# Four Strassen pairs for one merge gate, and a row moved between two stages

## The chip, the cores and the metric

The kernel runs on one core of a Trainium2 chip. The metric is the time of one execution on the device in microseconds (us), taken as the median of several runs. A core has five engines that run side by side and wait for each other through semaphores: TensorE (PE, the matmuls; its weight loads are listed as PEld), VectorE (DVE), ScalarE (ACT), GpSimd (POOL) and SyncE (SP), which here only issues transfers between HBM and the on-chip memory. PSUM, the memory that the matmuls write, has 8 banks of 128 x 512 fp32. The profile is of one execution on the chip, and gives each instruction's start and duration.

## The reference

One decoder layer, 1024 tokens of 1024 channels, all in fp32:

```
h = RMSNorm(x)
s5_x | s5_gate | lru_x | lru_gate | gate_s | gate_l = h @ W_in     (512, 512, 1280, 1280, 1024, 1024 columns)
y_s = S5(s5_x); y_s = GLU(GELU(y_s) @ W_glu) * silu(s5_gate);      z_s = y_s @ W_bs
y_l = RGLRU(conv4(lru_x)) * silu(lru_gate);                        z_l = y_l @ W_bl
x = x + RMSNorm((sigmoid(gate_s) * z_s + sigmoid(gate_l) * z_l) @ W_out)
x = x + (p @ W_ple) * sigmoid(x @ W_ple_gate)
```

S5 is a diagonal complex state space model; RGLRU is a gated recurrence in ten heads of 128 channels, whose gates are r and i, with a = exp(c r), a multiplier sqrt(1 - a^2), and a scan over the tokens.

## The kernel before

**Matmuls.** Channels lie on the 128 partitions, tokens along the rows, in two halves of 512. A weight block is 128 x 128. Every operand is split into a high part (a rounded copy, made by ScalarE) and a low part (the rest, made by VectorE as a subtraction), and one block product is three matmuls of 128 x 512 (`three`, lines 327 to 331): high x high, high weight x low data, low weight x high data. A *row* (`rows`) is one block of 128 output columns over all 8 blocks of 1024 input channels and both halves of the tokens: 48 matmuls. W_in has 44 such columns: 0 to 3 s5_x, 4 to 7 s5_gate, 8 to 17 lru_x, 18 to 27 lru_gate, 28 to 35 gate_s, 36 to 43 gate_l.

**Strassen pairs.** Two columns m and m+1 together with two halves of the inputs and two of the tokens are a 2 x 2 block product, which `lprod` and what follows do in seven products of 12 matmuls instead of eight. The first product (B11) and the second (B21) accumulate in one bank X; then come T2, T1, T3, B22 and T4 into banks Z and W. T1 to T4 are sums of quarters of h, each built once for all pairs by `t_early` and `t_build` (VectorE subtracts, ScalarE makes the high part, VectorE the low part). Before the change gate_s has three pairs, at columns 30, 32 and 34, and plain rows for 28 and 29. The products with W_bl further on have the same shape (`bprod`, banks bX, bZ, bW, bV), where W_bl's channels 8 and 9 (of ten) are not in the 2 x 2 scheme and are added as *tails* (`btail`).

**Weights.** `weight_plan` writes out the order of all weight blocks; SP loads chunks of eight in that order. A chunk is used as two *quads* of four blocks. `W.ahead()` makes quads some places ahead of the one in use, in a ring of six: high part by ScalarE (L232), low part by VectorE (L245), or, for the quads in `LIGHT`, by a second ScalarE copy (L236) and an adding transfer that GpSimd issues (L237). A row uses two quads, a Strassen product one.

**Order.** There is no planner. Each engine takes its instructions in the order in which the program writes them. Side work is written as generators in a list `bg`; `tick()` advances each of them by one step, four times in a row and once after a product, and `drain()` runs them to the end.

**The stages around the change.** Behind the norm come the rows for S5's input (u), then twelve plain rows (4, 5, 36 to 43, 28, 29), beside which the S5 model runs as side work (`s5_all`: eight blocks, each with a few small matmuls and a Gelu at its end, `py` and `ysb`). Then the three pairs. Then ten LRU heads: for each the row lru_x (conv), the row lru_gate (silu), and two gate products per half of the tokens, which `between` calls inside the next row. What follows a head's gates is its `late`: Tanh, Exp, Square, Sqrt on ScalarE, two products, the scan and the product with silu on VectorE, giving yr0 to yr9. Behind the heads come the s5_gate rows 6 and 7 (`light` with silu), which have head 9's gates inside and its `late` beside them; then yl8 and yl9 are split, and the W_bl products begin: four B11 products, the tails, four B21 products, then the GLU (`ps_eb`, `ps_ea`, whose input `geo` is split from S5's outcome), and the rest of the W_bl products. The B21 operand is the split of four of the yr rows (`bB`).

Of the kernel before, what the change touches and what calls it, by code (L numbers as in the profile page):

```python
# [34 lines left out]
PAIRS = (30, 32, 34)  # L35


def weight_plan():
# [46 lines left out]
    gated(6, NL - 1)  # L85
    plain(col("w_in", 7, range(ND)))
    hi2 = range(8, NL)
    for ks in (lo, hi2, hi):
# [175 lines left out]
def tile_hybrid_trunk(  # L264
# [81 lines left out]
    def drain():  # L346
        while bg:
            tick()
# [769 lines left out]
    for m in range(2):  # L1118
        light(4 + m, sil_d[m], True, ev_tile)
    for m in range(ND):  # L1120
        light(36 + m, sgl_d[m], False, ev_tile)
    for m in range(PAIRS[0] - 28):
        light(28 + m, sgs_d[m], False, ev_tile)
# [24 lines left out]
    def lprod(ps, op, start):  # L1148
        W.ahead()
        for k, wb in enumerate(W.next()):  # L1150
            three(ps, wb, (op[0][:, k, :], op[1][:, k, :]), start and k == 0, k == 3, not start)

# [3 lines left out]

    wide_ctx.close()
    gps = gctx.enter_context(tc.tile_pool(name="gps", bufs=1, space=PSUM))

    def gbank(i, name):  # L1160
        return gps.tile([P, HT], F32, tag=f"gb{i}", name=name)

    bg.append(t_build())
    lu = quarter(page(9, "lu", F32))
    xs = [px.tile([P, HT], F32, tag="px", name=f"lX{p_}") if p_ < 2 else gbank(0, "lX2") for p_ in range(3)]
    for p_ in range(3):
        if p_ == 0:
            tick()
        lprod(xs[p_], hq["B11"], True)
        S.activation(lu[:, p_], xs[p_], AF.Copy)  # L1170
        tick()
    for p_, m in enumerate(PAIRS):
        o = gp.tile([P, NT], F32, tag="c", name=f"lo{p_}", bufs=2)[:, HALF[0]]
        lprod(xs[p_], hq["B21"], False)
        gate_out(m, 0, o, xs[p_])
        tick()
    for p_, m in enumerate(PAIRS):
        z = gbank(1 + p_, f"lZ{p_}") if p_ < 2 else px.tile([P, HT], F32, tag="px", name="lZ2")
        w_ = gbank(3 + p_, f"lW{p_}")
# [47 lines left out]
    def lru_head(m):  # L1227
# [22 lines left out]
        def gates(h):  # L1250
            if h == 0:
                held.extend(W.next())
            for t, b, bias in ((r, held[0], b_a), (i, held[1], b_x)):
                ps = px.tile([P, HT], F32, tag="px", name=f"pg{m}{h}")
# [66 lines left out]
    def gel_build():  # L1321
        for _ in range(3):
            yield
# [22 lines left out]
    def b21_ops():  # L1346
        bop("B21", 0, 1)
        for k in range(4):
            bsplit("B21", k, bq(21, k))
            if k % 2:  # L1350
                yield
# [505 lines left out]
```

## Time and profile before

| | |
|---|---|
| median of three runs | 920.82 us (920.50 to 920.89) |
| the profiled execution, and its span | 920.58 us, 918.8 us |
| TensorE, matmuls | 911.0 us busy, 99%, 4192 records |
| VectorE, ScalarE, GpSimd | 71%, 54%, 13% busy |
| rows beside S5 | about 69 to 235 us |
| the three pairs | 235 to 293 us |
| LRU heads and rows 6 and 7 | 293 to 559.8 us |
| first W_bl products (B11, tails, B21) | 559.8 to 587.0 us |

A row of the timeline gives start, duration (both us), engine, line of the program, operation, the tile written and the tiles read, the shape, and how many instructions the row joins; in square brackets stands how long the engine was idle before, and what ended that. A row of the waits gives the engine and its instruction, what it waited for, us in total, times, and the longest. Buffer numbers are left out of the names in the profile: `wq` is every quad of weights in the ring, `wraw` every loaded chunk, `lX` and `bX` are the banks of the first two products, `sg` the outcome of a Sigmoid row, `bB` a split operand of a W_bl product. Line numbers in the profile are those of the kernel before.

### The profile page before, as it was taken

Reading aid. Unit: us, or ns where it says so; the run is one execution under the profiler, and the core shown is the slowest. Engines: PE = TensorE matmul, PEld = TensorE weight load, DVE = VectorE, ACT = ScalarE, POOL = GpSimd, SP = SyncE. Lnnn points to the kernel's source line nnn. Section 1 sums busy time; section 2 is a strip of 40 time slices with the busy share of each in tenths; the row PEclk is TensorE's granted clock in tenths of the full one; section 3 lists DMA queues with packets and bytes.
Section 4 is the critical chain, followed back from the end, with each engine's and each line's share of the span. In section 5 each row is a group of like instructions: output and inputs, shape, how many; then the busy total and the mean of one; then the engine's idle time right before and its main releaser. Section 6 shows DMA issues by size and latency. Waiting matters only on the chain.

```text
span 918.8 us, 11750 instructions
## 1 busy us (share of the span) xinstructions
PE 911.0 (99%) x4192; PEld 754.0 (82%) x4192; DVE 656.6 (71%) x1068; ACT 494.6 (54%) x764; POOL 116.8 (13%) x129
## 2 busy tenths in 40 slices
PE   9999999999999999999999999999999999999998
PEld 7888888888788888888888888888888887887887
DVE  6978978796762356667666668687762798886863
ACT  6644255456754257776666668445433345558531
POOL 1211000011100000000000000021322126422100
PEclk9999999999999999999999999999999999999999
DMA  9785777668455101111111117811579965499961
GB/s 357 296 269 154 220 239 198 187 180 244 127 172 172 52 29 34 47 51 52 51 48 52 51 46 232 284 35 57 164 265 230 274 156 206 126 249 235 275 206 57
DMA packets 76298, 146.53 MB, mean 159 GB/s; under 512 B 18896, under 2 KB 33360, under 8 KB 76240
## 3 DMA queue, kind: packets, MB, share of 16 engines
q1 hardware_dynamic: 53216, 110.39, 36.0%
q10 hardware_dynamic: 16256, 22.55, 8.3%
q0 software_dynamic: 6768, 12.85, 7.8%
q8 instruction: 33, 0.54, 0.2%
q14 instruction: 25, 0.20, 0.1%
HBM read 101.06 MB, written 31.72 MB: 145 GB/s over the span
## 4 chain that ended last, share of the span: by engine, by line
PE 84%; issue 9%; DVE 2%; DMA 2%; POOL 2%; ACT 1%; POOLq 0%; ACTq 0%; DVEq 0%
PE ps_L L331 10%; PE ps_rg L331 8%; PE ps_rx L331 8%; PE ps_L L329 5%; PE ps_rx L329 4%; PE ps_rg L329 4%; PE ps_pg L331 3%; PE ps_u L331 3%; PE bZ L331 3%; PE ps_F L331 3%; PE bW L331 2%; PE bX L331 2%; PE pg L331 2%; PE lZ L331 2%; PE ps_ple L331 2%
## 5 line engine op out<-in xcount | busy, mean ns | idle before, releaser
L331 PE MATMUL ps_L<-hB,wq 128*128 128x512 f32 x448 | 138.1, 389 | 0.0
L232 ACT ACTIVATE wq<-wraw 128x512 fp32r<-128x512 f32 (+1 forms) x191 | 114.8, 614 | 42.4 <-DMA wraw<-w_blocks 15.3
L245 DVE TENSOR_TENSOR wq<-wraw,wq 128x512 fp32r<-128x512 f32 (+1 forms) x146 | 100.6, 704 | 15.0 <-ACT wq L232 14.9
L331 PE MATMUL ps_rg<-hB,wq 128*128 128x512 f32 x320 | 98.6, 389 | 0.0
L331 PE MATMUL ps_rx<-hB,wq 128*128 128x512 f32 x320 | 98.5, 389 | 0.0
L331 PEld LDWEIGHTS ps_L<-hB,wq 128*128 128x128 f32 x448 | 84.1, 188 | 17.4
L329 PE MATMUL ps_L<-hB,wq 128*128 128x512 f32 x224 | 88.1, 393 | 0.0
L331 PE MATMUL ps_pg<-x1hl,wq 128*128 128x512 f32 x240 | 74.6, 391 | 0.7 <-DVE x1hl L1533 0.5
L1237 DVE SCALAR_TENSOR_TENSOR c<-ps_rx,cp_t,c 128x1023 f32<-128x1023 f32 (+2 forms) x30 | 38.4, 1282 | 49.2 <-ACT c L1235 48.5
L331 PEld LDWEIGHTS ps_rx<-hB,wq 128*128 128x128 f32 x320 | 60.1, 188 | 12.6
L331 PEld LDWEIGHTS ps_rg<-hB,wq 128*128 128x128 f32 x320 | 60.1, 188 | 12.6
L329 PE MATMUL ps_rx<-hB,wq 128*128 128x512 f32 x160 | 62.2, 389 | 0.0
L329 PE MATMUL ps_rg<-hB,wq 128*128 128x512 f32 x160 | 62.2, 389 | 0.0
L237 POOL DMA_DIRECT2D wq<-wraw x45 | 39.6, 880 | 163.5 <-ACT wq L236 118.0
L204 POOL TENSOR_TENSOR wS<-wraw 128x512 f32<-128x512 f32 x8 | 12.4, 1547 | 333.5 <-DMA wraw<-w_blocks 326.1
L331 PEld LDWEIGHTS ps_pg<-x1hl,wq 128*128 128x128 f32 x240 | 44.8, 188 | 11.3 <-DVE x1hl L1533 1.4
L329 PEld LDWEIGHTS ps_L<-hB,wq 128*128 128x128 f32 x224 | 42.1, 188 | 8.5
L329 PE MATMUL ps_pg<-x1hl,wq 128*128 128x512 f32 x120 | 46.9, 391 | 0.0
L331 PE MATMUL ps_u<-hB,wq 128*128 128x512 f32 x128 | 39.8, 392 | 0.4 <-DVE hB L771 0.4
L331 PE MATMUL ps_F<-ys,wq 128*128 128x512 f32 x128 | 39.4, 389 | 0.0
L1245 ACT ACT_TABLE_LOAD x9 | 11.5, 1283 | 51.2 <-DVE yr L1274 51.2
L329 PEld LDWEIGHTS ps_rg<-hB,wq 128*128 128x128 f32 x160 | 30.0, 188 | 6.2
(394 smaller groups left out, 2071.3 us busy)
## 6 DMA issues: line engine op xcount, KB each, us to landing
wraw<-w_blocks SPq DMA_DIRECT2D x98, 512.0 KB
wq<-wraw POOLq DMA_DIRECT2D x45, 256.0 KB, 4.8
xt<-x_t SPq DMA_DIRECT2D x8, 512.0 KB
ple_d<-ple_sb SPq DMA_DIRECT2D x8, 512.0 KB
h_d<-xt SPq DMA_DIRECT2D x8, 512.0 KB
wn<-sbt ACTq DMA_DIRECT2D x8, 512.0 KB
wn<-pt_d ACTq DMA_DIRECT2D x16, 256.0 KB
fT<-h_d ACTq DMA_DIRECT2D x4, 1024.0 KB
```

The costliest lines, as they stand in the source:

```text
L204: (self.nc.vector if light else G).tensor_tensor(s[name], s[a], s[b], op)
L232: nc.scalar.activation(hi, src, AF.Copy)
L237: nc.gpsimd.dma_start(lo.bitcast(F32), src, accum_op=ALU.add)
L245: self.nc.vector.tensor_tensor(lo, src, hi.bitcast(F32), ALU.subtract)
L329: T.matmul(ps, wh, xh, start=start, stop=False, skip_group_check=more)
L331: T.matmul(ps, a, b, start=False, stop=stop and a is (wh if xl_last else wl), skip_group_check=more)
L1237: V.scalar_tensor_tensor(c[:, d:], ps[:, :NT - d], w_[3 - d], c[:, d:], ALU.mult, ALU.add)
L1245: S.activation(sq, ps, AF.Sigmoid)
```

## The change

Columns 28 and 29 become a fourth pair. The first products (B11) of all four pairs are written before the `drain()` that ends the S5 side work, in the order of `PORDER` (columns 32, 34, 28, 30), with the banks of two pairs in one wide tile; the second products follow, with `t_build` beside them. The s5_gate row 6 moves from behind the LRU heads to the rows beside S5, so that eleven rows and four first products stand there where twelve rows stood. Behind the heads only row 7 is left. Both halves of head 9's gates now stand in the middle of that row, and the first W_bl products are reordered: B11, then B21, then the tails; the B21 operand and yl8, yl9 are split beside the B11 products, and S5's outcome beside the B21 products.

```
-PAIRS = (30, 32, 34)
+BESIDE = (4, 5, *range(36, 39), 6, *range(39, 44))
+PORDER = (2, 3, 0, 1)
+PAIRS = (28, 30, 32, 34)
...
-    for m in (4, 5, *range(36, 44), *range(28, PAIRS[0])):
+    for m in BESIDE:
         plain(col("w_in", m, range(ND)))
-    first = [b for ks in (lo, hi) for m in PAIRS for b in col("w_in", m, ks)]
+    first = [b for ks in (lo, hi) for i in PORDER for b in col("w_in", PAIRS[i], ks)]
...
-    gated(6, NL - 1)
-    plain(col("w_in", 7, range(ND)))
+    gated(7, NL - 1)
     hi2 = range(8, NL)
-    for ks in (lo, hi2, hi):
+    for ks in (lo, hi, hi2):
...
+    for p_ in PORDER:
+        if p_ < 2:
+            xs[p_] = px.tile([P, HT], F32, tag="px", name=f"lX{p_}")
+        lprod(xs[p_], hq["B11"], True)
+        for i in ((), (2, 3), (0,), (1,))[PORDER.index(p_)]:
+            S.activation(lu[:, i], xs[i], AF.Copy)
+        tick()
     drain()
     s5x.close()
...
+    bg.append(t_build())
+    for n, p_ in enumerate(PORDER):
+        lprod(xs[p_], hq["B21"], False)
+        for i in ((), (2, 3), (0,), (1,))[n]:
+            o = gp.tile([P, NT], F32, tag="c", name=f"lo{i}", bufs=2)[:, HALF[0]]
+            gate_out(PAIRS[i], 0, o, xs[i])
+        tick()
     wide_ctx.close()
...
+    def between(q):
+        if q == 0:
+            last(0)
+            last(1)
+
+    light(7, sil_d[3], True, lambda name: l1.tile([P, NT], F32, tag="c", name=name, bufs=2), between=between)
     gel_load()
...
+    def tail_ops():
+        tail_split(8)
+        yield
+        bop("B21", 0, 1)
+        for k in range(4):
+            bsplit("B21", k, bq(21, k))
+            if k == 1:
+                yield
+        while 9 not in yl_raw:
+            yield
+        tail_split(9)
+
+    bg.append(tail_ops())
+    bu = quarter(page(19, "bu", F32))
+    x01 = wide("bX01")
+    xs = [x01[:, HALF[p]] if p < 2 else px.tile([P, HT], F32, tag="px", name=f"bX{p}") for p in range(4)]
+    for p_ in range(4):
+        bprod(xs[p_], "B11", True)
+        for i in ((), (0, 1), (2,), (3,))[p_]:
+            S.activation(bu[:, i, :], xs[i], AF.Copy)
+        tick()
+    drain()
...
     for p_ in range(4):
-        bprod(xs[p_], "B11", True)
-        S.activation(bu[:, p_, :], xs[p_], AF.Copy)
+        bprod(xs[p_], "B21", False)
         tick()
...
             btail(xs[2 * q + i], wb[2 * i:2 * i + 2], 0, False)
-        tick()
-    for p_ in range(4):
-        bprod(xs[p_], "B21", False)
-        brow(2 * p_, 0, gts[p_ // 2][:, HALF[p_ % 2]], xs[p_])
+        for p_ in (2 * q, 2 * q + 1):
+            brow(2 * p_, 0, gts[p_ // 2][:, HALF[p_ % 2]], xs[p_])
         tick()
```

How the instructions move is shown at three places. The lists give the program's order on one engine, without times; a number behind a name counts the buffer, and line numbers are somewhat higher in the changed kernel (L232 is L233 there).

ScalarE at the end of S5, before the change. `ysb7` is S5's last Gelu, `sg_29` the Sigmoid of the last plain row, `wq` quads of weights (a light one in two copies), `lu` the copies of the first products:

```order
L1016 ACT_TABLE_LOAD
L1016 ACTIVATE ysb7_2289<-py7_2290 128x512
L1020 DMA y_d_84<-ysb7_2289 8x16x128 x4
L1065 ACT_TABLE_LOAD
L1065 ACTIVATE sg_29_2304<-ps_L29_2209 128x1024
L1069 DMA sgs_d_80<-sg_29_2304 128x1024
L232 ACTIVATE wq40_2325<-wraw22_1946 128x512
L236 ACTIVATE wq40_2325<-wraw22_1946 128x512
L1170 ACTIVATE lu_2317<-lX0_2318 128x512
L232 ACTIVATE wq41_2346<-wraw22_1946 128x512
```

And now:

```order
L1138 ACTIVATE lu_2212<-lX23_2213 128x512 x2
L1095 ACTIVATE lT20_2261<-fT2_2054 128x512 x4
L233 ACTIVATE wq40_2267<-wraw22_1949 128x512
L237 ACTIVATE wq40_2267<-wraw22_1949 128x512
L1138 ACTIVATE lu_2212<-lX0_2266 128x512
L233 ACTIVATE wq41_2290<-wraw22_1949 128x512
L237 ACTIVATE wq41_2290<-wraw22_1949 128x512
L1138 ACTIVATE lu_2212<-lX1_2289 128x512
L1017 ACT_TABLE_LOAD
L1017 ACTIVATE ysb7_2315<-py7_2316 128x512
L1021 DMA y_d_84<-ysb7_2315 8x16x128 x4
L233 ACTIVATE wq42_2336<-wS2_42_2300 128x512
```

The light quads and the copies of the first products now stand ahead of S5's last Gelu.

ScalarE at head 9's gates, before. `r9` and `i9` are the Sigmoids of the two gates (`pg90` the first half of the tokens, `pg91` the second), `sq9` the Sigmoid of the lru_gate row, `ta9` the Tanh that begins `late`:

```order
L1245 ACTIVATE sq9_4257<-ps_rg9_4341 128x1024
L232 ACTIVATE wq110_4418<-wraw60_4182 128x512
L1256 ACTIVATE r9_4254<-pg90_4445,cp_t_97 128x512
L1256 ACTIVATE i9_4255<-pg90_4450,cp_t_97 128x512
L232 ACTIVATE wq111_4455<-wraw61_4221 128x512
L1256 ACTIVATE r9_4254<-pg91_4484,cp_t_97 128x512
L1256 ACTIVATE i9_4255<-pg91_4489,cp_t_97 128x512
L1065 ACTIVATE sg_6_4494<-ps_L6_4417 128x1024
L232 ACTIVATE wq112_4499<-wraw61_4221 128x512
L232 ACTIVATE wq113_4501<-wraw62_4301 128x512
L1262 ACTIVATE ta9_4256<-r9_4254,sp8_98 128x1024
```

And now:

```order
L1249 ACTIVATE sq9_4336<-ps_rg9_4420 128x1024
L233 ACTIVATE wq115_4497<-wraw62_4261 128x512
L1263 ACTIVATE r9_4333<-pg90_4524,cp_t_97 128x512
L1263 ACTIVATE i9_4334<-pg90_4525,cp_t_97 128x512
L1263 ACTIVATE r9_4333<-pg91_4534,cp_t_97 128x512
L1263 ACTIVATE i9_4334<-pg91_4534,cp_t_97 128x512
L233 ACTIVATE wq116_4543<-wraw63_4300 128x512
L233 ACTIVATE wq117_4545<-wraw63_4300 128x512
L1269 ACTIVATE ta9_4335<-r9_4333,sp8_98 128x1024
```

The four gate Sigmoids follow one another, and row 6's Sigmoid is gone from here.

VectorE from there to the W_bl products, before. `i9` by `ta9`, the scan into `sq9`, and `yr9` are the end of head 9; `sg_7` is row 7's silu, `yl8` and `yl9` the tails' operands, `bB211` the low part of the B21 operand; wq111 to wq114 are the four B11 weights, wq117 is B21's first:

```order
L1267 SCALAR_TENSOR_TENSOR ta9_4256<-sq9_4257,ta9_4256 128x1024
L245 TENSOR_TENSOR wq113_4501<-wraw62_4301,wq113_4501 128x512
L1270 TENSOR_TENSOR i9_4255<-i9_4255,ta9_4256 128x1024
L1271 SCALAR_TENSOR_TENSOR sq9_4257<-r9_4254,i9_4255 128x1024
L1274 TENSOR_TENSOR yr9_4566<-sq9_4257,g9_4253 128x1024
L1067 TENSOR_TENSOR sg_7_4568<-sg_7_4568,ps_L7_4498 128x1024
L325 TENSOR_TENSOR yl8_4578<-yr8_4413,yl8_4578 128x1024
L325 TENSOR_TENSOR yl9_4581<-yr9_4566,yl9_4581 128x1024
L245 TENSOR_TENSOR wq114_4537<-wraw62_4301,wq114_4537 128x512
L325 TENSOR_TENSOR bB211_4619<-yr2_3749,bB210_4618 128x512 x2
```

And now, where wq114 to wq117 are the four B11 weights and wq118 and wq119 B21's first two:

```order
L1274 SCALAR_TENSOR_TENSOR ta9_4335<-sq9_4336,ta9_4335 128x1024
L1068 TENSOR_TENSOR sg_7_4581<-sg_7_4581,ps_L7_4496 128x1024
L246 TENSOR_TENSOR wq117_4545<-wraw63_4300,wq117_4545 128x512
L1277 TENSOR_TENSOR i9_4334<-i9_4334,ta9_4335 128x1024
L1278 SCALAR_TENSOR_TENSOR sq9_4336<-r9_4333,i9_4334 128x1024
L326 TENSOR_TENSOR yl8_4614<-yr8_4492,yl8_4614 128x1024
L246 TENSOR_TENSOR wq118_4595<-wraw64_4380,wq118_4595 128x512
L1281 TENSOR_TENSOR yr9_4634<-sq9_4336,g9_4332 128x1024
L326 TENSOR_TENSOR bB211_4637<-yr2_3828,bB210_4636 128x512 x2
L246 TENSOR_TENSOR wq119_4617<-wraw64_4380,wq119_4617 128x512
L326 TENSOR_TENSOR bB211_4637<-yr3_4161,bB210_4636 128x512 x2
L326 TENSOR_TENSOR yl9_4664<-yr9_4634,yl9_4664 128x1024
```

Row 7's silu and the last B11 weight now stand ahead of the scan, and the B21 operand's low parts stand behind it, with the tails no longer between B11 and B21 on TensorE.

More of the change, by code (lines that the diff above doesn't have):

```diff
@@ L1146, in t_build @@
         t_low("T4")
[L1148 to L1151, printed above, removed]
     def gate_out(m, h, t, src):
@@ L1327, in gel_build @@
             S.activation(t[:, 0], gel[b // 2][:, b % 2], AF.Copy)
-            yield
             V.tensor_tensor(t[:, 1], gel[b // 2][:, b % 2], t[:, 0].bitcast(F32), ALU.subtract)
             yield
-    def bprod(ps, name, start):
-        W.ahead()
-        hi, lo = bops[name]
-        for k, wb in enumerate(W.next()):
-            three(ps, wb, (hi[:, k, :], lo[:, k, :]), start and k == 0, k == 3, not start)
     def btail(ps, wb, h, start):
```

80 lines of the change are left out of this document (33 added, 47 removed).

## The prediction

> **What bounds the kernel now.** I read the page's first part, then what TensorE waited for, then TensorE's timeline at the places that the change touches.
>
> ```profile
> span 918.8 us, 11750 instructions
> PE 911.0 (99%) x4192; PEld 754.0 (82%) x4192; DVE 656.6 (71%) x1068; ACT 494.6 (54%) x764; POOL 116.8 (13%) x129
> ...
> PE lX L331 <- DMA wq<-wraw: 0.5, 1, 0.5
> PE oY L331 <- DVE wq L245: 0.3, 1, 0.3
> ```
>
> TensorE is occupied 99% of the span, and its longest wait between the start-up and 760 us is half a microsecond. So a matmul that is removed is worth its pace, and a wait that is added is paid in full: nothing behind it has slack in which PE could catch up. The pace and the stalls at the end of the S5 stage, from TensorE's timeline:
>
> ```profile
> 234.85 0.48 PE L329 MATMUL lX<-hB,wq 128*128 128x512 f32 x1
> ...
> 247.31 0.50 PE L331 MATMUL lX<-hB,wq 128*128 128x512 f32 x1 [0.48 <-DMA wq<-wraw]
> ...
> 252.47 0.39 PE L329 MATMUL lZ<-lT,wq 128*128 128x512 f32 x1
> ...
> 255.19 0.39 PE L329 MATMUL lW<-lT,wq 128*128 128x512 f32 x1
> ```
>
> A product is 4 blocks of 3 matmuls. One takes 255.19 - 252.47 = 2.72 us, 0.2267 us a matmul (the 0.39 in a row is a latency, and overlaps the next). The 72 matmuls of lX should take 16.32 us and take 252.47 - 234.85 = 17.62, so 1.30 us are lost there.
>
> **The change: the columns 28 and 29.** Plain, two columns cost 2 x 8 x 2 x 3 = 96 matmuls; as a pair they cost 7 products of 12, that is 84. 12 x 0.2267 = **2.72 us gained**.
>
> **The end of S5.** Why are 1.30 us lost now? ScalarE's order there:
>
> ```profile
> 235.14 0.60 ACT L1016 ACTIVATE ysb<-py 128x512 f32<-128x512 f32 x1 [3.49 <-PE py L1014]
> 235.76 2.46 ACTq L1020 DMA_DIRECT2D y_d<-ysb  x4
> ...
> 239.55 1.03 ACT L1065 ACTIVATE sg<-ps_L 128x1024 f32<-128x1024 f32 x1
> ...
> 244.04 2.19 ACT L1094 ACTIVATE lT<-fT 128x512 fp32r<-128x512 f32 x4
> ```
>
> It sits from py to 240.6 on a Gelu, four y_d issues, a table load and a Sigmoid, and the light weights come only then. In the changed order all eight light quads stand ahead of that Gelu, so I take 1.2 us of the 1.30 as **gained** (0.1 is the switch from the small S5 matmuls, which stays). Against it, the operands T1, T3, T4 are built in four ticks before the first T2 product where there were seven. Counting from the second products' start, the last two of them end at 8.2 and 10.9 and T2, T1, T3, B22 may start at 10.9, 13.6, 16.3 and 19.0. ScalarE: a Sigmoid behind 8.2, T1's high part (2.19, the row above) to 11.0; a weight, the Sigmoid behind 10.9, T3's high part to 14.1; two copies for the last weight, one of Z, T4's high part to 17.7; a weight and the copy of W to 18.7. VectorE splits T1 and T3 right behind these (to 11.7 and 16.9, block by block, each block ahead of its matmul), and adds on W from 18.7 to 19.4. B22 writes W and waits for that: **0.4 us lost**; bounds 0 (if ScalarE is 0.4 earlier) and 2.7 (if one operand misses by a product). The fourth pair's own sums and copies are those of the three pairs that run without a wait now.
>
> **The silu row in S5.** It brings one VectorE multiply of 1.22 us and a store on SP, and its multiply stands ahead of a scan and waits for a Sigmoid. In the same place now:
>
> ```profile
> 156.38 1.03 ACT L1065 ACTIVATE sg<-ps_L 128x1024 f32<-128x1024 f32 x1
> ...
> 157.27 1.36 DVE L988 TENSOR_TENSOR_SCAN q<-r,q 128x128 f32<-128x128 f32 x4
> ...
> 161.31 0.42 DVE L1003 TENSOR_TENSOR q<-ta,tb 64x254 f32<-64x254 f32 x1
> ...
> 165.69 0.38 PE L1013 MATMUL py<-U,toep 128*128 128x128 f32 x2
> ```
>
> The scan would start at 157.41 + 1.2 + 0.6 (a weight's low part) = 159.2, so q is done 1.9 us later, at 163.6. The next S5 output product, which reads q, begins at 165.69, so this costs nothing; with that cover gone it would be 1.9. The row's 48 matmuls only change place.
>
> **The start of the w_bl products.** This is where I expect the loss. Now row 7 and the four B11 products lie between the last gates and the tails, and B21 comes after the tails:
>
> ```profile
> 540.78 0.39 PE L329 MATMUL pg<-chl,wq 128*128 128x512 f32 x1
> ...
> 548.95 0.39 PE L329 MATMUL ps_L<-hB,wq 128*128 128x512 f32 x1
> ...
> 559.83 0.39 PE L329 MATMUL bX<-bB,wq 128*128 128x512 f32 x1
> ...
> 576.14 0.39 PE L329 MATMUL bX<-bB,wq 128*128 128x512 f32 x1
> ```
>
> On this clock (all of it shifts alike) the change has 12 gate matmuls from 540.78 to 543.50, the second half of the only row to 548.94, B11 products from there, each 2.72, to 559.82, and then at once B21. B21 is thus wanted at 559.8, not at 576.1: 16.3 us earlier. How much earlier can its operands be? ScalarE now:
>
> ```profile
> 543.24 1.03 ACT L1245 ACTIVATE sq<-ps_rg 128x1024 f32<-128x1024 f32 x1
> 544.16 0.62 ACT L232 ACTIVATE wq<-wraw 128x512 fp32r<-128x512 f32 x1
> 544.68 0.68 ACT L1256 ACTIVATE r<-pg,cp_t 128x512 f32<-128x512 f32 x1
> 545.25 0.69 ACT L1256 ACTIVATE i<-pg,cp_t 128x512 f32<-128x512 f32 x1
> ...
> 551.68 1.15 ACT L1262 ACTIVATE ta<-r,sp 128x1024 f32<-128x1024 f32 x1
> ...
> 557.69 1.06 ACT L1268 ACTIVATE ta<-ta 128x1024 f32<-128x1024 f32 x1
> ...
> 559.29 1.28 ACT L1065 ACT_TABLE_LOAD   x1
> 560.59 1.03 ACT L1065 ACTIVATE sg<-ps_L 128x1024 f32<-128x1024 f32 x1
> ```
>
> Up to 544.68 nothing changes. Then come four gate Sigmoids (0.57 apart: to 546.97), two weights (0.52 each) and the Tanh at 548.0: only 3.7 us earlier than 551.68. From Tanh to Sqrt stays 6.01 (554.0), then the table load and row 7's Sigmoid, 1.06 + 1.30 later, 556.4 to 557.4. VectorE's steps behind that, now:
>
> ```profile
> 558.79 1.22 DVE L1270 TENSOR_TENSOR i<-i,ta 128x1024 f32<-128x1024 f32 x1 [0.55 <-ACT ta L1268]
> 560.04 2.29 DVE L1271 TENSOR_TENSOR_SCAN sq<-r,i 128x1024 f32<-128x1024 f32 x1
> 562.37 1.23 DVE L1274 TENSOR_TENSOR yr<-sq,g 128x1024 f32<-128x1024 f32 x1
> 563.51 1.21 DVE L1067 TENSOR_TENSOR sg<-sg,ps_L 128x1024 f32<-128x1024 f32 x1
> 564.64 2.35 DVE L325 TENSOR_TENSOR yl<-yr,yl 128x1024 fp32r<-128x1024 f32 x2
> 566.92 0.68 DVE L245 TENSOR_TENSOR wq<-wraw,wq 128x512 fp32r<-128x512 f32 x1
> 568.64 1.30 DVE L325 TENSOR_TENSOR bB<-yr,bB 128x512 fp32r<-128x512 f32 x2 [1.04 <-ACT bB L324]
> ```
>
> The new order is: row 7's multiply (waits for 557.4; 1.14), the low part of the *last B11 weight* (0.68, ready at **559.3**), i by ta (1.25), the scan (2.3), the split of yl8 (1.15), a weight (0.6), yr9 (1.14), and only then B21's first low part, ready at 559.2 + 1.25 + 2.3 + 1.15 + 0.6 + 1.14 + 0.68 = **566.3**. TensorE's third matmul of the last B11 product is due at 557.10 + 0.45 = 557.55 and waits 1.75 us. B21's second matmul, due at 561.8 by then, waits for 566.3: 4.5 us. B21's third low part comes behind one more weight, at 568.1, where 567.7 would do: 0.4. Each restart costs some 0.12 more. **7.0 us lost.** What stands behind VectorE's queue meanwhile (weights of the second and third B21 products, yl9, geo) has a product or more of room, since PE is late too. SP is held too: row 7's store waits for 558.6 with the first GLU weights behind it (wanted at 583), and the gate loads wait for the heads' buffers to 569.7 (wanted at 580). Bounds: 0, if VectorE got to these parts in time, and 8.5, if each of the eight steps is 0.2 slower beside ScalarE's.
>
> **Sum.** 920.58 (the profiled execution) - 2.72 - 1.2 + 0.4 + 7.0 = 924.06. The median shown is 0.24 above that execution, so 924.3.
>
> **Rivals.** *The clock falls behind the long wait.* Between two matmuls of B21 PE does nothing for 4.3 us; no wait of such length lies behind the start-up in this trace, so it cannot say what follows. What a slow clock costs it shows at the start:
>
> ```profile
> 5.38 0.77 PE L329 MATMUL ps_ple<-p_hi,wq 128*128 128x512 f32 x1 [0.54 <-ACT wq L232]
> ...
> 7.25 0.63 PE L329 MATMUL ps_ple<-p_hi,wq 128*128 128x512 f32 x1
> ...
> 9.38 0.57 PE L331 MATMUL ps_ple<-p_lo,wq 128*128 128x512 f32 x1
> ```
>
> Five matmuls from 7.25 to 9.38 are 0.426 each, 0.2 over the pace, in a stretch of 4.0 us (5.38 to 9.38). The same stretch once more would lose 9.4 x 0.2 = 1.9 us: 926.2. The Trainium skill ("TensorE: Matmul & The Clock Gate", Part 1: The HAM clock gate) says that the clock is halved after an idle window of about 3.4 us, whose phase is free, so that 4.3 us may or may not hold a whole one. By that rule a new wait of this size costs more than its length; no run here shows it yet.
>
> *VectorE makes it in time.* Then the 7.0 fall away: 917.06 + 0.24 = 917.3, faster. For it: VectorE is busy only 71%. Against it: what counts is the order, and B21's parts would have to be ready 4.5 us sooner, and ScalarE's chain from the gates to row 7's Sigmoid holds no wait that the change takes away. It decides from 561.8 on.
>
> *Only the first wait comes.* If the B21 parts slip ahead but the last B11 weight does not, 1.75 + 0.12 are lost: 919.2, within the noise.
>
> *An operand at S5's end misses by a product* (T1 or T3, the 2.7 above in place of 0.4): 924.3 + 2.3 = 926.6. For it: three ticks fewer; against it: T1's and T3's low parts come out 1 to 2 us ahead of use in my count.
>
> **How the numbers follow.** The forecast, 924.3, has 0.56 (its own range 922.8 to 925.6); the clock 0.20; the late operand 0.06; only the first wait 0.10; VectorE in time 0.08. A measurement of this kernel tells about 0.2%, 1.84 us, from no change. So faster 0.08, same 0.10, slower 0.82. The range, 921.8 to 927.2, leaves out the two cases below and takes in the others and their bounds.
>
> **What would show it.** TensorE's waits should list bX for VectorE's wq (about 1.8) and for bB (about 4.5), and the lX wait should be gone; PE instructions fall by 12. In VectorE's timeline the bB split should start some 8 us after row 7's multiply. If a row between the start-up and the bX products shows a new wait, the S5 part is wrong; if bX has no wait of a microsecond, the whole sign is. If the matmuls after it stand 0.43 apart, the clock rival holds.

## The result, and the profile after

The changed kernel takes **932.44 us** (median of 4 runs, 931.56 to 933.12), the kernel before 920.85 beside it. Beside the later runs the kernel before took 920.5 to 921.4, so the ratios compare better than the medians. The ratio is 1.0126, with a 95% interval of 1.0109 to 1.0144: slower, as forecast, but by 11.6 us where 3.5 were forecast, and above the range of 921.8 to 927.2.

The first lines of the page and the longest of TensorE's waits between the start-up and the GLU, after the change (a wait's row gives us in total, times, and the longest):

```profile
span 930.1 us, 11766 instructions
PE 912.9 (98%) x4180; PEld 753.5 (81%) x4180; DVE 661.6 (71%) x1075; ACT 499.3 (54%) x775; POOL 119.4 (13%) x132
...
PE bX L332 <- DVE bB L326: 4.1, 1, 4.1
PE lZ L330 <- ACT lu L1189: 2.6, 1, 2.6
PE bX L332 <- DVE wq L246: 1.6, 1, 1.6
```

TensorE has the 12 records less that were counted (4180 against 4192), and yet is 1.9 us longer "busy": part of its matmuls ran on a slower clock. The two bX rows are the ones the prediction named. The lZ row is not: it lies at S5's end, where the prediction had only 0.4 us; a new wait there was its sign that the S5 part is wrong.

**The w_bl products.** TensorE there, and VectorE's rows that set it:

```profile
572.95 0.51 PE L332 MATMUL bX<-bB,wq 128*128 128x512 f32 x1 [1.63 <-DVE wq L246]
579.86 1.22 PE L332 MATMUL bX<-bB,wq 128*128 128x512 f32 x2 [4.08 <-DVE bB L326]
```

```profile
571.07 1.22 DVE L1068 TENSOR_TENSOR sg<-sg,ps_L 128x1024 f32<-128x1024 f32 x1 [3.49 <-ACT sg L1066]
572.21 0.68 DVE L246 TENSOR_TENSOR wq<-wraw,wq 128x512 fp32r<-128x512 f32 x1
...
574.06 2.29 DVE L1278 TENSOR_TENSOR_SCAN sq<-r,i 128x1024 f32<-128x1024 f32 x1
...
579.12 1.28 DVE L326 TENSOR_TENSOR bB<-yr,bB 128x512 fp32r<-128x512 f32 x2
```

The last B11 weight's low part stands right behind row 7's multiply, and B21's first low part 579.12 - 571.07 = 8.05 us behind that multiply. With the restarts the two waits cost 1.8 and 4.25 us. The third wait of the prediction (0.4) does not show: that low part is ready at 580.93 + 0.68 = 581.61, and the matmul that reads it starts at 582.59. On the full clock it would have been due at 579.86 + 6 x 0.227 = 581.22, so the slow clock hid it.

**S5's end.** TensorE from the second products (234.89) to the first pair's T4 (263.25):

```profile
234.89 0.48 PE L330 MATMUL lX<-hB,wq 128*128 128x512 f32 x1
...
246.24 0.50 PE L330 MATMUL lZ<-lT,wq 128*128 128x512 f32 x1 [0.21 <-ACT lo L1165]
...
255.15 0.65 PE L330 MATMUL lZ<-lT,wq 128*128 128x512 f32 x1 [2.58 <-ACT lu L1189]
...
263.25 0.47 PE L330 MATMUL lZ<-lT,wq 128*128 128x512 f32 x1 [0.75 <-DVE lc L1196]
```

The lX stalls of before are gone: four second products take 10.88 us at 2.72 each, and T2 follows them at 246.24, 0.5 us late. But T4, which four further products (T2, T1, T3, B22) would let start at 234.89 + 8 x 2.72 = 256.65, starts at 263.25: **6.6 us lost**. ScalarE shows why:

```profile
223.70 1.03 ACT L1066 ACTIVATE sg<-ps_L 128x1024 f32<-128x1024 f32 x1
228.09 0.34 ACTq L1070 DMA_DIRECT2D sgl_d<-sg  x1
228.47 0.63 ACT L233 ACTIVATE wq<-wraw 128x512 fp32r<-128x512 f32 x1 [3.74 <-DMA wraw<-w_blocks]
...
243.81 1.28 ACT L1165 ACT_TABLE_LOAD   x1 [1.38 <-DMA y_d<-ysb]
...
247.82 0.60 ACT L1165 ACTIVATE lo<-lX 128x512 f32<-128x512 f32 x1 [1.11 <-DMA sgs_d<-lo]
248.31 2.18 ACT L1095 ACTIVATE lT<-fT 128x512 fp32r<-128x512 f32 x4
...
254.52 0.58 ACT L1189 ACTIVATE lu<-lZ 128x512 f32<-128x512 f32 x1
```

Three waits for transfers stand in its queue: 3.4 us to issue the store of the last plain row (the Sigmoid ends at 224.73, the store goes out at 228.09, once a chunk of weights has landed), 1.4 us for S5's y_d stores before the first Sigmoid lo, whose buffer lies where S5's tiles lay, and 1.1 us for the third lo, whose buffer still has the first one to store: 5.9 us together. T1's high part, the first lT here, starts at 248.31.

### The profile page after: what moved, and what is told of

Same layout as the page of the kernel before. It is cut to its first block, busy times and chain, and to the rows that moved or that the text cites. A ratio compares the mean times of both kernels' runs of the same rounds, so it can differ in the third digit from the quotient of the medians.

```text
span 930.1 us, 11766 instructions
## 1 busy us (share of the span) xinstructions
PE 912.9 (98%) x4180; PEld 753.5 (81%) x4180; DVE 661.6 (71%) x1075; ACT 499.3 (54%) x775; POOL 119.4 (13%) x132
## 4 chain that ended last, share of the span: by engine, by line
PE 76%; issue 8%; DVE 5%; ACT 5%; DMA 3%; POOL 2%; ACTq 0%; POOLq 0%; DVEq 0%; SPq 0%
PE ps_rx L332 8%; PE ps_L L332 7%; PE ps_rg L332 7%; PE ps_rx L330 4%; PE ps_L L330 4%; PE ps_rg L330 4%; PE ps_u L332 3%; PE bZ L332 3%; PE ps_F L332 3%; PE ps_pg L332 2%; PE lZ L332 2%; PE bW L332 2%; DMA wq<-wraw 2%; PE pg L332 2%; PE ps_ple L332 2%
## 5 line engine op out<-in xcount | busy, mean ns | idle before, releaser
L233 ACT ACTIVATE wq<-wraw 128x512 fp32r<-128x512 f32 (+1 forms) x192 | 115.5, 614 | 47.9 <-DMA wraw<-w_blocks 18.0
L332 PE MATMUL ps_L<-hB,wq 128*128 128x512 f32 x384 | 118.4, 390 | 0.0
L332 PEld LDWEIGHTS ps_L<-hB,wq 128*128 128x128 f32 x384 | 72.1, 188 | 15.0
L330 PE MATMUL ps_L<-hB,wq 128*128 128x512 f32 x192 | 75.7, 394 | 0.0
L238 POOL DMA_DIRECT2D wq<-wraw x48 | 42.2, 879 | 187.3 <-ACT wq L237 124.9
L330 PEld LDWEIGHTS ps_L<-hB,wq 128*128 128x128 f32 x192 | 36.1, 188 | 7.2
```

Of the source, the lines that this page charges most:

```text
L233: nc.scalar.activation(hi, src, AF.Copy)
L238: nc.gpsimd.dma_start(lo.bitcast(F32), src, accum_op=ALU.add)
L330: T.matmul(ps, wh, xh, start=start, stop=False, skip_group_check=more)
L332: T.matmul(ps, a, b, start=False, stop=stop and a is (wh if xl_last else wl), skip_group_check=more)
```

## The experiments

To compare places in the traces I add up, from the starts of consecutive matmuls, what each gap over 0.25 us has beyond the pace of 0.227; a matmul on the halved clock (0.427 apart) counts 0.2, in a sum of its own. "S5's end" goes from the first lX to the first `ps_rx`, "w_bl" from the first bX to the first `ps_eb`.

| kernel | median (range), us | ratio to before (95%) | S5's end: waits + halved clock | w_bl: waits + halved clock |
|---|---|---|---|---|
| before | 920.82 (920.50 to 920.89) | 1 | 1.2 + 0 | 0 + 0 |
| the change | 932.44 (931.56 to 933.12) | 1.0126 (1.0109 to 1.0144) | 4.8 + 1.7 | 6.0 + 1.6 |
| tail_alone | 927.95 (927.10 to 929.77) | 1.0075 (1.0058 to 1.0092) | 0 + 0 | 6.0 + 2.6 |
| tail_mult | 927.05 (926.58 to 928.17) | 1.0070 (1.0055 to 1.0085) | 5.1 + 1.6 | 2.3 + 1.5 |
| tail_split | 932.16 (931.67 to 933.79) | 1.0127 (1.0112 to 1.0142) | 5.0 + 1.6 | 5.1 + 2.5 |
| front_store | 930.31 (928.73 to 930.58) | 1.0100 (1.0085 to 1.0115) | 4.8 + 0 | 6.3 + 1.5 |
| tail_fix | 928.60 (927.74 to 929.38) | 1.0087 (1.0072 to 1.0102) | 4.0 + 1.6 | 3.3 + 1.6 |
| front_halves | 927.02 (926.52 to 927.89) | 1.0071 (1.0056 to 1.0086) | 4.7 + 0 | 4.3 + 0 |
| front_subs | 928.40 (927.16 to 929.05) | 1.0084 (1.0068 to 1.0099) | 4.9 + 1.6 | 4.3 + 0 |
| front_all | 924.13 (923.57 to 924.23) | 1.0037 (1.0023 to 1.0052) | 0.9 + 0 | 3.0 + 1.7 |
| tail_free | 925.07 (924.34 to 925.71) | 1.0048 (1.0033 to 1.0063) | 6.0 + 0 | 1.3 + 0 |
| all_fixed | 919.90 (919.20 to 920.69) | 0.9991 (0.9982 to 1.0000) | 0.9 + 0 | 1.3 + 0 |
| all_fixed2 | 920.09 (919.96 to 921.28) | 0.9993 (0.9984 to 1.0002) | 1.3 + 0 | 1.3 + 0 |
| all_fixed3 | 918.30 (917.75 to 918.69) | 0.9965 (0.9951 to 0.9978) | 0.9 + 0 | 0.1 + 0 |

The code at S5's end is the same in the change, tail_mult, tail_split, tail_fix and tail_free, and their profiles give 6.5, 6.7, 6.6, 5.5 and 6.0 us there: differences of a microsecond in this column alone carry nothing.

### The tail alone (tail_alone)

The kernel before, with row 6 beside S5 and the changed order from head 9's gates on; three pairs with their first products behind the `drain()` as before, and 28 and 29 stay plain. Against the change:

```
-BESIDE = (4, 5, *range(36, 39), 6, *range(39, 44))
-PORDER = (2, 3, 0, 1)
-PAIRS = (28, 30, 32, 34)
+BESIDE = (4, 5, *range(36, 39), 6, *range(39, 44), 28, 29)
+PAIRS = (30, 32, 34)
...
```

> The kernel before (three pairs, columns 28 and 29 plain), but with the silu row 6 among the rows beside S5 and with the changed order from head 9's gates on. Theory (the start of the w_bl products costs what the changed kernel's trace shows there: waits of 1.8, 4.25 and 0.4, two restarts, and 1.4 to 1.6 for the halved clock behind the long wait; the silu row costs nothing): 920.85 + 8.0 to 8.5, so 928.9 to 929.4, with bX waiting for wq (1.8) and bB (4.2), and no new wait between 60 and 290 us. Rival (the moved silu row makes S5 end late, and that is part of what the first pair lost): some 2 us more, 931, with a new wait around 156 to 166 us or at S5's end.

Measured: 927.95, 7.1 us over the 920.82 of before, and 1.0075 (1.0058 to 1.0092) beside it. The profile has the two bX waits of the change, and no wait over 0.1 us from 60 to 300 us:

```profile
569.09 0.50 PE L331 MATMUL bX<-bB,wq 128*128 128x512 f32 x1 [1.63 <-DVE wq L245]
...
576.00 1.22 PE L331 MATMUL bX<-bB,wq 128*128 128x512 f32 x2 [4.13 <-DVE bB L325]
```

So the silu row among the S5 rows costs nothing, and the loss at the w_bl products does not come from the pairs. The time is about a microsecond below the expectation. The profiled execution, whose clock was halved for two windows (2.6 in the table), took 929.77 at a mean granted clock of 0.995; the other three took 927.1 to 928.2 at 0.996 to 0.998. The 1.2 us of lX stalls are gone here too, though no product stands beside S5, so the extra row alone removes them. The rival, S5 ending late, falls.

### What holds B21: row 7's multiply, or head 9's chain (tail_mult, tail_split)

Two kernels, each the change with one edit. tail_mult takes row 7's Sigmoid, multiply and store out of the way: they become a generator in `bg` that acts in the fourth tick of the B11 products, behind the last of the four (the expectation says the third; three `yield`s make it the fourth). tail_split moves the split of B21 itself, from `tail_ops` to behind the gates.

```
-    light(7, sil_d[3], True, lambda name: l1.tile([P, NT], F32, tag="c", name=name, bufs=2), between=between)
+    ps7 = rows(hplain, "L7", between=between)
+
+    def silu7():
+        yield
+        yield
+        yield
+        t = l1.tile([P, NT], F32, tag="c", name="sg_7", bufs=2)
+        S.activation(t, ps7, AF.Sigmoid)
+        V.tensor_tensor(t, t, ps7, ALU.mult)
+        nc.sync.dma_start(sil_d[3], t)
```

```
     def between(q):
         if q == 0:
             last(0)
             last(1)
+            bop("B21", 0, 1)
+            for k in range(4):
+                bsplit("B21", k, bq(21, k))
```

> The changed kernel, but row 7's Sigmoid, multiply and store are written behind the third B11 product instead of ahead of the first. Theory (ScalarE's Sigmoid and VectorE's multiply of row 7 hold back the last B11 weight's low part, and then head 9's chain and the B21 splits behind it): the 1.8 us wait for wq goes; VectorE begins head 9's chain 3 to 4 us earlier, so the wait for bB falls from 4.25 to about 2, which leaves the clock alone: 5 to 6 us faster than the changed kernel, 926.5 to 927.5. Rival (what holds B21 is head 9's own chain, Tanh to scan; the multiply only costs the first wait): the bB wait grows by what the first wait gave, the clock falls as before: 0 to 1 us faster, 931.5 to 932.4.

> The changed kernel, but the B21 operand is split right behind head 9's gates, ahead of head 9's chain, instead of behind its scan. Theory (row 7's multiply comes first on VectorE, and four more copies ahead of Tanh make it 2.4 us later): bX waits about 4 for the last B11 weight, and about 2.5 for the first B21 weight's low part behind the scan; the wait for bB is gone; sum 6 to 7 against 6.3, so no gain: 931.5 to 933. Rival (the wait for bB was the cost, and the wait for wq stays at 1.8): 4.2 and the clock's 1.5 gained, 926.5 to 927.

Measured: tail_mult 927.05, 5.4 us faster than the change; tail_split 932.16, no gain. Both as the theory had it. Their longest bX waits:

```profile
575.86 0.74 PE L332 MATMUL bX<-bB,wq 128*128 128x512 f32 x2 [1.98 <-DVE bB L326]
```

```profile
574.75 0.79 PE L332 MATMUL bX<-bB,wq 128*128 128x512 f32 x1 [3.71 <-DVE wq L246]
```

With the multiply gone, the wait for the weight is gone and B21's is 2.0 in place of 4.1: everything behind the multiply moved up. With the split moved but the multiply left, the wait for bB is gone and the wait for the weight has grown from 1.6 to 3.7, because four more copies stand ahead of Tanh, and with it ahead of row 7's Sigmoid. (The second wait of 2.5 that the theory had there was 1.2, at a later weight, behind two halved windows.) What the theory had wrong is the clock: it was to stay full behind a wait of 2 us, and was halved all the same (below). The profiled execution of tail_mult gains 3.7 us over that of the change (931.83 to 928.17), less than the medians do. It had two halved windows, and a mean granted clock of 0.996; the other three took 926.6 to 927.4 at 0.998 to 0.999. One halved window is 3.41 x 0.5 / 926 = 0.002 of that mean, so some of them had a halved window less: the clock differs between executions of one kernel.

### The tail's order, repaired in two steps (tail_fix, tail_free)

tail_fix has both edits, and head 9's last product and scan two ticks later:

```
+            if m == NL - 1:
+                yield
+                yield
             V.tensor_tensor(i, i, ta, ALU.mult)
             V.tensor_tensor_scan(sq, r, i, 0.0, ALU.mult, ALU.add)
```

tail_free has besides every weight's low part ahead of a tick of the B11 products, row 7's Sigmoid one tick earlier, the split of yl8 two ticks later, and geo2 and geo3 two ticks later:

```
         for i in ((), (0, 1), (2,), (3,))[p_]:
             S.activation(bu[:, i, :], xs[i], AF.Copy)
+        W.lows(len(W.done) - 1)
         tick()
```

> The changed kernel with both edits at its tail: row 7's Sigmoid and multiply behind the third B11 product, the B21 operand split right behind head 9's gates, and besides head 9's last product and scan two ticks later. Theory (the w_bl products' start lost about 8 us to VectorE's order alone): no bX wait over 0.5 us, no halved clock there, 8 us faster than the changed kernel: 924 to 925. Rival (the tails then wait for yr9, whose scan comes later, or a weight's low part behind the scan holds B21): a new wait of 1 to 3 us at 560 to 575 us, 926 to 928.

> tail_fix, and its 2.7 us wait (the last B21 weight's low part behind yr9's split and row 7's multiply) removed by order: every weight's low part ahead of the side work of its tick, row 7's Sigmoid and multiply and the split of yl8 behind the third B11 product, half of S5's outcome split behind the first tails. Theory (the w_bl products' start cost 1.8 + 4.3 + 0.4 + restarts 0.25 + about 1.5 of halved clock = 8.2, all by VectorE's order): no bX wait over 0.3 us, 8 us faster than the changed kernel: 924 to 925. Rival (the work of ScalarE and VectorE does not fit beside these products in any order, so the wait goes to the GLU's first product): a wait of 1 to 2.5 us at 585 to 592 us, 925.5 to 927.

Measured: tail_fix 928.60, 3.8 us faster than the change and 4 us short of the theory: the two waits are gone, but yr9's split and row 7's multiply now stand behind the last B11 product, and the last B21 weight's low part behind them comes 2.5 us late; the rival's kind of wait, at another product. tail_free takes that away: 925.07, 7.4 us faster than the change, and what is left is one wait of a tail for its weight:

```profile
584.89 0.50 PE L332 MATMUL bX<-yl,wq 128*128 128x512 f32 x1 [1.04 <-DVE wq L246]
```

So about 7.5 us of the change's loss lie at the w_bl products, and order alone makes and removes them; no instruction was saved.

### ScalarE at S5's end (front_store, front_halves, front_subs, front_all)

front_store is the change with one store on SP:

```
-        (nc.sync if silu else nc.scalar).dma_start(dst, t)
+        (nc.sync if silu or wm == BESIDE[-1] else nc.scalar).dma_start(dst, t)
```

front_halves is tail_fix, with two lo tiles in one buffer:

```
-            o = gp.tile([P, NT], F32, tag="c", name=f"lo{i}", bufs=2)[:, HALF[0]]
-            gate_out(PAIRS[i], 0, o, xs[i])
+            if i % 2 == 0:
+                lo = gp.tile([P, NT], F32, tag="c", name=f"lo{i}", bufs=2)
+            gate_out(PAIRS[i], 0, lo[:, HALF[i % 2]], xs[i])
```

front_subs is tail_fix, with the differences in `t_early`, and `t_build` left with T1's high part in its first tick (in page 2, which S5's memory doesn't touch), T1's low and T3's high in the third, T3's low and T4's high in the fourth:

```
         t_low("T2")
+        yield
+        t_subs("T3", "T2", "T3")
+        yield
+        t_subs("T4", "T4", "T2")
...
-    lop = {"T2": [3, 19], "T1": [16, 17], "T3": [15, 2], "T4": [7, 8]}
+    lop = {"T2": [3, 19], "T1": [2, 16], "T3": [15, 17], "T4": [7, 8]}
```

front_all is tail_fix with all three.

> The changed kernel, but the store of the last plain row beside S5 (column 43) is issued by SP instead of ScalarE; ScalarE there waited 3.4 us to issue it (from 224.7 to 228.1). Theory (that wait made ScalarE late at S5's end, and all later operands with it): ScalarE's Sigmoids lo, the high parts of T1, T3, T4 and the copy lu come 2.5 to 3.5 us earlier, the 2.75 us wait of lZ for lu goes, and the halved clock at 255 us with it; 4.5 to 5.5 us faster than the changed kernel, 927 to 928. Rival 1 (ScalarE is held at S5's end by waits for stores to land, and only moves up to those): less than 1.5 us faster, 931 to 932. Rival 2 (the four ticks in place of seven, VectorE's order): no gain, 932.4.

> tail_fix, and the four lo tiles use two buffers as halves, so that the third no longer waits 1.1 us for the first one's store. Theory (from T1's high part on, ScalarE and VectorE need 14.9 us up to T4's first matmul, in the changed kernel and in front_store alike, where TensorE would need 8.2; so all that makes T1's high part earlier by x gains x, and the halved clock at 255 us is hidden behind them): T1's high part 1.1 us earlier, 1.0 to 1.2 us faster than tail_fix. Rival (the halved clock counts there): if it goes, 2.5 us faster; else 1.1.

> tail_fix, and the differences T3 and T4 (2.49 us of VectorE each) are formed at S5's end, and T1, T3, T4 are split one tick or two earlier; T1's high part lies in a page that need not wait for S5's stores. Theory (ScalarE and VectorE have more to do per product of the first pair than the 2.72 us of TensorE): the work that stood beside the second products is less, T4 starts about 3 us earlier; 2.5 to 3.5 us faster than tail_fix. Rival (only the waits of ScalarE for stores at S5's end count, which stay): no more than 1 us faster.

> tail_fix with front_halves, front_subs and the store of column 43 on SP. Theory: the waits of lZ, lW at S5's end fall from 6.3 us to about 1 in sum: 5 to 6 us faster than tail_fix, and 3 us faster than the kernel before: 917.5 to 919. Rival (the three remedies overlap: each shortens the same wait): 3 us faster than tail_fix, 921 to 922.

**front_store**, 930.31: 2.1 us faster than the change, between theory and its first rival. ScalarE took the light weights 3.7 us earlier, ran into the next wait, and T1's high part came only 1.57 us earlier; T4's start moved by the same 1.56:

```profile
224.79 0.62 ACT L233 ACTIVATE wq<-wraw 128x512 fp32r<-128x512 f32 x1
...
242.24 1.28 ACT L1165 ACT_TABLE_LOAD   x1 [2.23 <-DMA wraw<-w_blocks]
...
246.74 2.18 ACT L1095 ACTIVATE lT<-fT 128x512 fp32r<-128x512 f32 x4
```

```profile
261.69 0.47 PE L330 MATMUL lZ<-lT,wq 128*128 128x512 f32 x1 [1.27 <-DVE lc L1196]
```

From T1's high part to T4's start it is 261.69 - 246.74 = 14.95 us here and 263.25 - 248.31 = 14.94 in the change, though TensorE waits at other places in between and though the clock was halved in the change and not here. So this stretch is a chain of ScalarE and VectorE alone. tail_free gives the same, on a full clock, with the order of the change: 262.18 - 247.24 = 14.94.

```profile
247.24 2.18 ACT L1095 ACTIVATE lT<-fT 128x512 fp32r<-128x512 f32 x4
```

```profile
262.18 0.47 PE L330 MATMUL lZ<-lT,wq 128*128 128x512 f32 x1 [1.24 <-DVE lc L1196]
```

VectorE's side of the chain, in the change: behind T1's low part stand three steps for coming weights before the add into Z, and T3's low part is ahead of the add into W, T4's ahead of the add into lc.

```profile
251.44 0.69 DVE L246 TENSOR_TENSOR wq<-wraw,wq 128x512 fp32r<-128x512 f32 x1
252.04 0.69 DVE L205 TENSOR_TENSOR wS<-wraw 128x512 f32<-128x512 f32 x1
252.77 0.69 DVE L205 TENSOR_TENSOR wS<-wS,wraw 128x512 f32<-128x512 f32 x1
253.37 0.69 DVE L1188 TENSOR_TENSOR lZ<-lZ,lu 128x512 f32<-128x512 f32 x1
253.97 2.49 DVE L1090 TENSOR_TENSOR lT<-fT,lT 128x512 fp32r<-128x512 f32 x4
...
258.21 0.70 DVE L1193 TENSOR_TENSOR lW<-lW,lu 128x512 f32<-128x512 f32 x1 [1.15 <-ACT lc L1192]
258.82 2.49 DVE L1090 TENSOR_TENSOR lT<-fT,lT 128x512 fp32r<-128x512 f32 x4
...
262.43 0.68 DVE L1196 TENSOR_TENSOR lc<-lc,lZ 128x512 f32<-128x512 f32 x1
```

**front_halves**, 927.02: 1.6 us faster than tail_fix by the medians, 0.8 by the sums at S5's end. Counted from the first lX, T1's high part comes 1.07 us earlier (246.23 - 222.20 against 247.04 - 221.94) and T4 1.04 (261.19 - 222.20 against 261.97 - 221.94), as the theory has it. The halved clock of tail_fix is gone here, and the rival's 2.5 did not come with it. **front_subs**, 928.40: 0.2 faster, so the theory (2.5 to 3.5) falls and its rival holds. T1's high part came out 5 us earlier (at 242.26), but ahead of the first two Sigmoids lo on ScalarE; these then hold the bank that T2 needs, and the third lo, T3's high part and lu behind them came no earlier:

```profile
247.41 0.50 PE L330 MATMUL lZ<-lT,wq 128*128 128x512 f32 x1 [1.15 <-ACT lo L1166]
...
256.31 0.50 PE L330 MATMUL lZ<-lT,wq 128*128 128x512 f32 x1 [3.17 <-ACT lu L1190]
```

**front_all**, 924.13: 4.5 us faster than tail_fix. The sum at S5's end falls from 5.5 to 0.9, one wait for lu of 0.6 and its restart, which is what the theory expected of this place. Its time of 917.5 to 919 was missed, since it counted from a tail_fix of 924 to 925. (An S5 product at 217 us waited 0.7 us for its `toep` loads in this profile; left open.) So no single remedy takes the loss away. I read it so: work that had room in seven ticks stands in four, in two queues almost without a pause, and each remedy alone only moves ScalarE up to the next thing that it waits for. No run removes the three waits and leaves the order as it is, so how much of the loss is theirs alone is not shown.

### Both ends (all_fixed, all_fixed2, all_fixed3)

all_fixed is front_all's S5 end with tail_free's tail. all_fixed2 calls `W.ahead()`, and with it the next weights' sums, behind the add into Z for the first pair:

```
-        lprod(z, lop["T2"], True)
+        lprod(z, lop["T2"], True, bool(p_))
         V.tensor_tensor(z, z, u, ALU.add)
         S.activation(u, z, AF.Copy)
+        if not p_:
+            W.ahead(2)
```

all_fixed3 has T4's low part two ticks later in `t_build`, and the tails' weights' low parts ahead of the ticks of the B21 products:

```
         lpage("T4", 1)
         yield
+        yield
+        yield
         t_low("T4")
...
         bprod(xs[p_], "B21", False)
+        W.lows(len(W.done) - 1)
         tick()
```

> front_all with tail_free's tail in place of tail_fix's. Theory (the two stages' losses add up, and what is left at S5's end is lZ's wait for lu, 0.7 to 1 with its restart): 920.7 - 2.72 - 1.2 + 1.0 = 917.8, at most 0.7 more if the S5 step at 216 us waits again. Rival (the removed waits come back further on, where geo or the gate loads are late): 919.5 to 921.

> all_fixed, and for the first pair VectorE's add into Z and ScalarE's copy of it stand ahead of the next weights' sums instead of behind them. Theory (VectorE's three weight steps of 0.6 us ahead of that add are what lZ still waits for): lZ's wait for lu goes, 0.7 to 0.9 faster than all_fixed: 917. Rival (T4's parts or the weights' sums, now later, hold B22 or the second pair's T2 instead): same as all_fixed or up to 1 slower.

> all_fixed2, and T4's low part is formed behind VectorE's adds into W and lc instead of ahead of them, and the tails' weights get their low parts ahead of S5's split. Theory (the last two waits that the change brought, 0.9 us of lW for VectorE's add and 1.0 us of bX for a weight, are again places in VectorE's queue): both go, all of the 2.72 and most of the 1.3 are kept: 917.5 to 918.5. Rival (VectorE has no room left for them, so T4 or the GLU's first product waits instead): 919.5 to 920.5.

Measured: all_fixed 919.90, level with the kernel before (0.9982 to 1.0000), 2.1 above the theory. Of that, 1.2 is the tail's wait for a weight that tail_free showed already, with its restart; another 0.7 is at the program's end (below). all_fixed2 took lZ's wait away and got one of lW in its place, for the same VectorE queue: no gain, its rival. all_fixed3 puts both VectorE queues in the order in which TensorE uses what they make: **918.30, 0.35% faster than the kernel before** (0.9965, 0.9951 to 0.9978), faster than both kernels; and in the list of its waits none for a Strassen or w_bl operand or weight is left (most of the 0.9 at S5's end is an S5 product's wait of 0.4 for its `toep` loads, and its restart). The page's first lines:

```profile
span 916.7 us, 11770 instructions
PE 908.3 (99%) x4180; PEld 751.5 (82%) x4180; DVE 660.9 (72%) x1075; ACT 499.2 (54%) x775; POOL 118.3 (13%) x132
```

## Why the prediction was right and wrong

**The sign and its reason were right.** The waits were to be 1.75, 4.5 and 0.4 with 0.12 for each restart, 7.0 in all; 1.8 and 4.25 were measured with their restarts, at the matmuls named, for the producers named. The 0.4 does not show, by the working above because the slow clock hid it, so the waits come to 6.05. And bB stood 8.05 us behind row 7's multiply where some 8 were said. tail_mult and tail_split show that the order said was the cause: the multiply first, the chain behind it.

**The 2.72 and the 1.2 were right, as a sum.** 12 records less, no lX wait. The reason given for the 1.2, the light quads ahead of S5's last Gelu, was not needed: in tail_alone the row alone takes these stalls away. all_fixed3, in which the new waits are gone, is 920.58 - 918.45 = 2.1 us below before in the profiled executions. Taking 2.72 and 1.2 from before, and adding the 1.0 that is left of waits and the 0.7 at the program's end, gives 2.2.

**The silu row's nothing was right** (tail_alone).

**The step that failed is "The end of S5": "0.4 us lost; bounds 0 and 2.7".** It measured 6.5. My count from the start of the second products had T1's high part end at 11.0; it ended at 248.31 + 2.18 - 234.89 = 15.6, so 4.6 late. And it had T4 start at 22.1, that is 13.3 behind the start of T1's high part (8.8), where the chain takes 14.9: 1.6 more. Together 6.2, of a T4 that is 263.25 - 234.89 - 22.1 = 6.3 late. Behind the 4.6 stand ScalarE's three waits for transfers. They sum to 5.9; by my estimate from the rows the rest, 1.3, was room that ScalarE had ahead of S5's last Gelu and of the third lo. The runs take away parts of it only: front_store moves T1's high part up by 1.57, front_halves by 1.07; none takes away all three alone. I had listed what ScalarE computes and not what it issues: the store of the last plain row stands in its queue ahead of all the light weights, and the stretch of its order that I looked at begins behind it. The 1.6 I put down to the weights' sums and low parts on VectorE and the light weights' second copies on ScalarE, which I had set beside TensorE's products and not in the two queues; all_fixed2 and all_fixed3, which move just such steps, take the last waits away. The upper bound of 2.7, one operand late by one product, was no bound: the operands come from one queue, so a late start makes all of them late. The rival with 0.06, one operand late by one product, had the place right, but its 2.3 over the 0.4 is too small too: 6.1 came.

**The clock rival, 0.20, held**, and at two places. At the w_bl products the eight matmuls of the halved window, 0.427 apart, cost 1.6, near the 1.9 of the prediction. How much of it is paid in the change no run shows. In kernels with the tail of tail_fix it is 0.6: from the first bX to the first `ps_eb` it takes 593.41 - 561.25 = 32.16 us in tail_fix, with a halved window, and 592.06 - 560.52 = 31.54 in front_halves without one, where the GLU's first product waits 0.9 us for VectorE. At S5's end it cost nothing, since the chain of 14.94 us sets the end there with a halved clock and with a full one.

**The sum.** Profiled, the change is 931.83 - 920.58 = 11.25 slower. Of that -2.72 and -1.2 are the gains, +6.5 is S5's end, +7.6 the w_bl products with their clock, +0.7 the program's end; 0.4 is not placed. That 7.6 is near the term's 7.0 is partly luck: the waits alone are 6.05, and the 1.6 of the clock was not in the term. Against the forecast of 3.5 over the profiled execution, 6.1 of the miss is S5's end. The range ended at 927.2 because that term's upper end did.

## What to carry to other kernels

Before an order is costed by sums, write out each engine's whole queue over the stretch, with the stores it issues and the low parts and sums it makes for later work, and start the list at the last thing that the engine surely finishes in time, not at the first line that the change touches. An operand that must be ready first must also be first in its engine's queue; where one queue feeds several products, a late start shifts all of them, so the bound is the shift and not one product. A remedy should be judged with the others in place: by the sums at S5's end front_store and front_halves gave 1.7 and 0.8 us and front_subs nothing, but the three together 4.6; and with all in, small moves of order gave another 1.6 by the medians, 1.2 by the sums.

## What the runs showed of the hardware

**The halved clock goes by fixed windows of 3.41 us, and a window need not be idle.** The windows view gives TensorE's busy time in a stretch (and its matmuls), then the granted clock. In the change, with stretches laid so that they end where the clock changes (PE alone):

```profile
251.93:255.34 3.41, 0.82 (x4) 1.00 0.70 221
255.34:258.76 3.42, 3.42 (x9) 0.50 0.45 86
576.20:579.61 3.41, 0.00 (x0) 1.00 0.00 0
579.61:583.02 3.41, 3.16 (x8) 0.50 0.25 59
```

The two halved stretches start 579.61 - 255.34 = 324.27 us apart, 95 times 3.413. The first comes behind a wait of only 2.6 us. In front_store (all engines; the first pair of numbers is PE) and in tail_mult:

```profile
572.68:576.09 3.41, 1.54 (x7) 0.94 (x5) 3.41 (x3) 2.86 (x6) 0.00 (x0) 1.00 0.54 175
576.09:579.51 3.42, 1.18 (x5) 1.00 (x6) 3.42 (x6) 1.80 (x3) 0.00 (x0) 1.00 0.00 0
579.51:582.92 3.41, 3.41 (x10) 2.25 (x9) 3.41 (x5) 3.38 (x6) 0.00 (x0) 0.50 0.57 160
```

```profile
573.63:577.04 3.41, 1.43 (x7) 0.99 (x6) 3.41 (x6) 2.98 (x6) 0.00 (x0) 1.00 0.00 0
577.04:580.45 3.41, 3.41 (x10) 2.26 (x9) 3.41 (x5) 3.38 (x5) 0.00 (x0) 0.50 0.49 154
```

Among the windows on the full clock behind the start-up, in all the traces here, one with 1.43 us or less of busy TensorE was followed by a halved one, one with 1.54 or more by a full one; in tail_mult a single wait of 2.0 us was enough. For a window that is itself halved the limit is higher: in tail_alone one with 1.88 us busy, and in tail_split one with 1.71, was followed by a second halved one.

```profile
574.46:577.88 3.42, 1.88 (x5) 1.49 (x6) 3.42 (x6) 2.50 (x5) 0.00 (x0) 0.50 0.00 0
577.88:581.29 3.41, 3.41 (x10) 2.64 (x8) 3.41 (x5) 2.63 (x5) 0.00 (x0) 0.50 0.72 181
```

Each time the clock came back after one or two windows. So the same wait can go either way by where it lies on the grid. tail_free waits 2.6 us for lu at the same place as the change does, but there the wait falls across two windows (laid by the clock's change at that program's end), and the clock stays:

```profile
249.79:253.20 3.41, 1.69 (x8) 1.07 (x6) 3.38 (x7) 3.41 (x8) 0.00 (x0) 1.00 0.46 126
253.20:256.61 3.41, 2.54 (x11) 2.12 (x12) 2.78 (x5) 3.41 (x8) 0.85 (x1) 1.00 0.68 181
```

The Trainium skill ("TensorE: Matmul & The Clock Gate", Part 1: The HAM clock gate) gives the free-running window of 3413 ns, and the trace agrees. Its "after ≥1 idle window" fits the change's w_bl products (0.00 us busy) and is too strict for tail_mult, where the window before was 42% busy (1.43 of 3.41).

**The program's end.** From the issue of the last store to the end it takes 918.8 - 915.98 = 2.8 us before the change and 930.1 - 926.56 = 3.5 after:

```profile
915.98 0.33 SPq L1775 DMA_DIRECT2D out_t<-sbp  x1
```

```profile
926.56 0.33 SPq L1794 DMA_DIRECT2D out_t<-sbp  x1
```

tail_alone, with three pairs, ends like before (4.6 us after the start of its last matmul), and the kernels with four pairs end 5.3 after it (front_store 5.0). The store and its data are the same; why its end takes longer was not tried.
